# Two layers in split fp32: high and low halves joined into 512-column products, and a wider pace for layer b's attention

## The chip, the cores and the metric

The kernel runs on one core of a Trainium2 chip. The metric is the device time of one execution in microseconds (us). Engines: PE is TensorE (PEld its weight loads), DVE is VectorE, ACT is ScalarE, SP is SyncE, whose queue issues the transfers.

## What is computed

Two residual layers over 256 tokens of width 2048, 16 heads of 128. Layer a is latent attention, layer b block attention, which with 256 tokens is one causal block with a linear distance penalty.

```python
def reference(x, ...):
    for i in range(2):                       # layer a, then layer b
        y = mixer_i(rms_norm(x, norm_i)) @ w_out_i
        x = x + y
    return x

def moba_mixer(h, w_in, q_norm, k_norm):     # layer b
    q, k, v, gate = jnp.split(h @ w_in, 4, axis=-1)
    q, k = rms_norm(heads(q), q_norm), rms_norm(heads(k), k_norm)
    o = softmax(q @ k.T * scale - slope * distance, causal) @ v
    return from_heads(o) * jax.nn.silu(gate)
```

Layer a (`mla_mixer`) has the same form with low-rank projections for q, k and v, and a gate from its own input projection.

## The kernel before

All data is fp32. A product of fp32 accuracy is made of three fast ones: each operand is split into a high part (`fp32r`, ScalarE) and a low part (the rest, VectorE), and high x high, high x low and low x high are summed in PSUM. Weights arrive in tiles of 128 x 1024 (`wr`, 512 KB), which ScalarE turns into `wh` and VectorE into `wl`; four raw tiles, four high and three low ones are held. The tokens' parts lie in `xh` and `xl` (input chunks of 128 features x 256 tokens), those of the attention output in `ogh` and `ogl` (one chunk per head).

Two kinds of projection block exist. `blk_rows` keeps tokens stationary and streams 512 (or 384) weight columns: q, k and v. `blk_cols` keeps 128 weight columns stationary and streams the 256 tokens: gates and output projections. There, each 128 output columns and each input chunk take three products of 256 columns, and two such outputs share one PSUM bank. Five banks (`acc`) serve the blocks in turn, three (`w`) the attention pieces.

Layer b runs in four groups of four heads: gate, q, k and v blocks of 512 columns each, 16 steps per block. When q and k are done they are normalized and transposed (`flip`: a VectorE copy, a transposing DMA on SP's queue, a second VectorE copy). Each head has three steps: `s1` (scores `ps_s`, softmax: VectorE's reduction into `sm`, ScalarE's exponential, reciprocal `ri`, scaling of `sm`), `s2` (a flip of the probabilities through `pz`, then `ph`, `pl`, `p1`) and `s3` (product with v into `ps_o`, VectorE's `og` with the gate, then ScalarE's high and VectorE's low part). The group before runs its `s1` to `s3` between the products of the next group; the last group's stand between the products of the output projection, whose input chunk i needs head i. The blocks of columns 0 to 511 and 512 to 1023 go first: 12 steps of one and 6 of the other (heads 0 to 11 only), then the rest.

The order on every engine is fixed when the kernel is built. `ordered` walks the main list (projection steps) and the side list (attention steps) by estimated costs, lags and three PSUM banks, and takes whichever is ready; a step that takes a bank comes at the earliest `PACE` = 600 ns after the last such one. Each engine then runs its own instructions in that order. `token_scale` makes layer b's norm: `ps_st` sums squares, VectorE takes the inverse root in some fifteen small operations, `ps_r` spreads it over the rows; the gates' evictions need the result.

Of the kernel before, what the change touches and what calls it, by code (L numbers as in the profile page):

```python
# [28 lines left out]
P = 128  # L29
# [20 lines left out]
PACE = 600  # L50
# [42 lines left out]
def trunk(ctx: ExitStack, tc, xT, gains, cst, w_in_a, w_q_up, w_kv_up, w_out_a, w_in_b, w_out_b, outT):  # L93
# [60 lines left out]
    class Step:  # L154
# [3 lines left out]
        def __init__(self, fn, cost=0, lag=0, needs=(), after=(), w=None, bank=False):  # L158
            self.fn, self.cost, self.lag, self.w, self.bank = fn, cost, lag, w, bank
            self.needs, self.after, self.end = list(needs), list(after), None  # L160
# [6 lines left out]
    def ordered(main, side):  # L167
# [4 lines left out]
        while main or side:  # L172
            can = []
            for s in side + main[:1]:
                r = s.ready()
                if r is not None:
                    can.append((max(r, min(banks), last + PACE) if s.bank else r, s))
            r, s = next(((r, s) for r, s in can if r <= now), None) or min(can, key=lambda x: x[0])
            (main if main and s is main[0] else side).remove(s)
            now = max(now, r) + s.cost  # L180
            s.end = now
            if s.bank:
                banks[banks.index(min(banks))] = now + HOLD
                last = now
            out.append(s)
# [17 lines left out]
    def blk_rows(w, x, done, lag=PB, first=()):  # L203
# [4 lines left out]
        def go(wt, c, k):  # L208
            xh, xl = x()
# [13 lines left out]
    def blk_cols(w, x, done, lag=3000):  # L223
# [4 lines left out]
        def go(wt, c, k):  # L228
            xh, xl = x()
# [13 lines left out]
        return _steps(w, go, 3 * ns * 109, lag)  # L243

# [116 lines left out]
    def gate_done(g, rows):  # L361
        def done(a):
            for b in range(len(a)):
# [47 lines left out]
    def head_steps(h, scores, bias, vt, cost, needs, needs_v, after, lag, front):  # L411
# [176 lines left out]
    x_a = lambda: (xh, xl)  # L588
# [130 lines left out]
    def out_done_a(j):  # L719
        def f(a):  # L720
            xt = res["x"]
            c = 2 * j
            both = lines(xt[:, c:c + 2].rearrange("p a b -> p (a b)"))
            nc.vector.tensor_tensor(both, unpaired(a[0]), both, op=ALU.add)  # L724
# [12 lines left out]
    og = lambda: (ogh, ogl)  # L737
    outs_a = [blk_cols(w_out_a[:, 256 * j:256 * (j + 1)], og, out_done_a(j), 4000) for j in range(8)]
# [31 lines left out]
    def group_b(g):  # L770
# [63 lines left out]
        gate = blk_cols(w(3), x_b, gate_done(2 * g, rows_b))  # L834
# [7 lines left out]
        for h in range(4):  # L842
            hb.append(head_steps(4 * g + h, scores(h), bias(4 * g + h), lambda h=h: [x[:, h] for x in z["v"]],
                                 545, [tq, tk], v[-1:] + gate[-1:], [], S2B, nc.vector.tensor_copy))
        gate[-1].after += [h[2] for h in old] + [row_b]
# [4 lines left out]
        else:  # L850
            for i, s in enumerate(gate):
                s.needs.append(outs_a[i // 2][-1])
# [5 lines left out]
    def out_done_b(j):  # L858
        def f(a):
            xt = res["x"]  # L860
            for b in range(2):
                c = 4 * j + 2 * b
                y = xt[:, c:c + 2]
                both = lines(y.rearrange("p a b -> p (a b)"))
                nc.vector.tensor_tensor(both, unpaired(a[b]), both, op=ALU.add)  # L865
                nc.sync.dma_start(outT[c * P:(c + 2) * P].rearrange("(c p) t -> p c t", p=P), y)
        return f

    outs_b = [blk_cols(w_out_b[:, 512 * j:512 * (j + 1)], og, out_done_b(j)) for j in range(4)]
# [9 lines left out]
    main += outs_b[0][:12] + outs_b[1][:6] + outs_b[0][12:] + outs_b[1][6:] + outs_b[2] + outs_b[3]  # L879
# [62 lines left out]
```

## Time and profile before

| what | value |
|---|---|
| median of 3 runs | 756.62 us (755.7 to 757.58) |
| profiled execution | 756.45 us, span 754.7 us |
| TensorE busy | 745.3 us, 99% of the span |
| VectorE busy | 576.7 us, 76% |
| ScalarE busy | 488.7 us, 65% |
| TensorE clock granted | 0.999 of full speed |
| moved by DMA | 153.19 MB, 203 GB/s on average |

The span runs from the first to the last instruction of the program; the execution's own time is 1.75 us longer. Matmuls are pipelined, so busy time sums overlapping records: paces are read from start to start, or from the pieces of the chain that ended last.

### The profile page before, as it was taken

To read this page: it belongs to the slowest core of one execution; us is meant where nothing else is said; L and a number is where in the kernel's file an instruction comes from. 1 tells how busy PE (TensorE), PEld (TensorE's weight loads), DVE (VectorE), ACT (ScalarE), POOL (GpSimd) and SP (SyncE) were. 2 spreads that over 40 slices of the span, in tenths; PEclk is the share of its full clock that TensorE was granted. 3 is DMA by queue.
4 is the path that set the end of the run, shared out by engine and by line. 5 is a ranking of instruction groups with operands and counts; after the bars stand their busy time and mean duration, and the time that the engine had idled before them with its cause. 6 is when DMAs were issued, how large, how long until landed. Compare 5 with 4: busy or idle time off the path is not lost.

```text
span 754.7 us, 14125 instructions
## 1 busy us (share of the span) xinstructions
PE 745.3 (99%) x5246; PEld 707.1 (94%) x5246; DVE 576.7 (76%) x1207; ACT 488.7 (65%) x1025; POOL 0.2 (0%) x4
## 2 busy tenths in 40 slices
PE   8999999999999999999999999999999999999997
PEld 7999999999999999998889988998889988899997
DVE  6888899999998596765787767886788857887552
ACT  7767888888877575445666556675567666674331
POOL 0000000000000000000000000000000000000000
PEclk9999999999999999999999999999999999999999
DMA  9866666666657966666877768876787677877761
GB/s 296 263 182 182 169 184 161 184 170 158 182 178 192 280 209 211 195 181 211 227 224 187 194 216 228 246 187 195 203 237 219 190 215 214 235 197 219 232 223 43
DMA packets 137973, 153.19 MB, mean 203 GB/s; under 512 B 47280, under 2 KB 94768, under 8 KB 137904
## 3 DMA queue, kind: packets, MB, share of 16 engines
q1 hardware_dynamic: 137760, 152.27, 70.4%
q8 instruction: 41, 0.67, 0.4%
q14 instruction: 28, 0.23, 0.1%
q10 hardware_dynamic: 144, 0.02, 0.0%
HBM read 139.68 MB, written 2.10 MB: 188 GB/s over the span
## 4 chain that ended last, share of the span: by engine, by line
PE 91%; DVE 4%; DMA 2%; ACT 1%; issue 1%; SPq 0%; DVEq 0%; ACTq 0%
PE acc L198 84%; PE ps_s L198 4%; DVE wl L150 2%; PE ps_o L198 2%; PE ps_ta L201 1%; DMA c_sb<-cst 1%; DMA wr<-w_in_a 1%; ACT wh L146 1%; DMA sm<-pz 0%; ACT sq L542 0%; DVE xt L724 0%; SPq L132 0%; PE ps_lt L201 0%; DVE xt L865 0%; DVE xl L314 0%
## 5 line engine op out<-in xcount | busy, mean ns | idle before, releaser
L146 ACT ACTIVATE wh<-wr 128x1024 fp32r<-128x1024 f32 (+3 forms) x265 | 287.9, 1091 | 161.8 <-PE acc L198 134.9
L150 DVE TENSOR_TENSOR wl<-wr,wh 128x1024 fp32r<-128x1024 f32 (+3 forms) x265 | 314.3, 1189 | 90.3 <-PE acc L198 58.1
L198 PE MATMUL acc<-wh,xh 128*128 128x512 f32 (+1 forms) x448 | 169.0, 377 | 1.2 <-ACT wh L146 1.2
L198 PE MATMUL acc<-wl,xh 128*128 128x512 f32 (+1 forms) x448 | 167.7, 374 | 0.8 <-DVE wl L150 0.8
L198 PE MATMUL acc<-wh,xl 128*128 128x512 f32 (+1 forms) x448 | 167.4, 374 | 0.0
L198 PE MATMUL acc<-xh,wh 128*128 128x256 f32 x512 | 142.3, 278 | 0.0
L198 PE MATMUL acc<-ogh,wh 128*128 128x256 f32 x512 | 142.0, 277 | 0.0
L198 PE MATMUL acc<-ogh,wl 128*128 128x256 f32 x512 | 141.0, 275 | 0.3 <-DVE wl L150 0.2
L198 PE MATMUL acc<-xh,wl 128*128 128x256 f32 x512 | 140.8, 275 | 0.0
L198 PE MATMUL acc<-ogl,wh 128*128 128x256 f32 x512 | 140.8, 275 | 0.0
L198 PE MATMUL acc<-xl,wh 128*128 128x256 f32 x512 | 140.8, 275 | 0.0
L198 PEld LDWEIGHTS acc<-ogh,wl 128*128 128x128 f32 x512 | 98.3, 192 | 0.7 <-DVE wl L150 0.7
L198 PEld LDWEIGHTS acc<-xl,wh 128*128 128x128 f32 x512 | 98.2, 192 | 0.3
L198 PEld LDWEIGHTS acc<-xh,wh 128*128 128x128 f32 x512 | 98.2, 192 | 0.3
L198 PEld LDWEIGHTS acc<-xh,wl 128*128 128x128 f32 x512 | 98.3, 192 | 0.0
L198 PEld LDWEIGHTS acc<-ogl,wh 128*128 128x128 f32 x512 | 98.3, 192 | 0.0
L198 PEld LDWEIGHTS acc<-ogh,wh 128*128 128x128 f32 x512 | 98.3, 192 | 0.0
L198 PEld LDWEIGHTS acc<-wh,xh 128*128 128x128 f32 x448 | 85.0, 190 | 11.9 <-ACT wh L146 1.9
L198 PEld LDWEIGHTS acc<-wl,xh 128*128 128x128 f32 x448 | 84.9, 190 | 11.4 <-DVE wl L150 1.3
L198 PEld LDWEIGHTS acc<-wh,xl 128*128 128x128 f32 x448 | 84.8, 189 | 10.3
L198 PE MATMUL acc<-wh,xt 128*128 128x384 f32 (+1 forms) x192 | 57.5, 357 | 0.0
L426 ACT ACTIVATE sm<-sm,mn 128x128 f32<-128x128 f32 x64 | 29.0, 455 | 11.3 <-DVE mn L424 11.3
(154 smaller groups left out, 833.5 us busy)
## 6 DMA issues: line engine op xcount, KB each, us to landing
wr<-w_in_b SPq DMA_DIRECT2D x128, 512.0 KB, 4.3
wr<-w_in_a SPq DMA_DIRECT2D x32, 512.0 KB, 4.1
wr<-w_out_a SPq DMA_DIRECT2D x32, 512.0 KB, 4.5
wr<-w_out_b SPq DMA_DIRECT2D x32, 512.0 KB, 4.6
wr<-w_in_a SPq DMA_DIRECT2D x15, 416.0 KB, 5.2
wr<-w_q_up SPq DMA_DIRECT2D x16, 384.0 KB, 3.8
wr<-w_kv_up SPq DMA_DIRECT2D x8, 512.0 KB, 3.8
xt<-xT SPq DMA_DIRECT2D x4, 512.0 KB, 5.5
```

The lines of the kernel that those rows point to most:

```text
L146: nc.scalar.activation(self.ordering(self.h)[1], self.ordering(self.raw)[0], AF.Copy)
L150: nc.vector.tensor_tensor(self.ordering(self.l)[1], self.ordering(self.raw)[0], self.ordering(self.h.bitcast(F32))[1], op=ALU.subtract)
L198: chain(nc.tensor.matmul(*args, skip_group_check=True, **kw))
L201: chain(nc.tensor.transpose(*args))
L426: nc.scalar.activation(sm[:, sl], sm[:, sl], AF.Exp, bias=mn[:, t:t + 1], scale=-1.0, accum_out=rs[:, t:t + 1])
```

## The change

The tokens' high and low parts now lie side by side in one tile (`xhl`, `ohl`: 256 high columns, then 256 low ones). A new block, `blk_both`, streams both in one product of 512 columns with the high weights, and the high half alone with the low weights: two products for three, the same columns in all. An output of 128 columns now fills a PSUM bank, high half and low half apart, which are added when it is evicted (`gate_done` with `halves`, `added`). It is used for layer b's gates (in two pieces of 256 columns for one of 512), for the last four output pieces of layer a (pieces 4 to 7) and for the output columns 1024 to 1791 of layer b, whose last 256 columns stay with `blk_cols`. Layer b's attention steps get a pace of 3500 ns.

```diff
-        def __init__(self, fn, cost=0, lag=0, needs=(), after=(), w=None, bank=False):
+        def __init__(self, fn, cost=0, lag=0, needs=(), after=(), w=None, bank=False, pace=PACE):
...
-                    can.append((max(r, min(banks), last + PACE) if s.bank else r, s))
+                    can.append((max(r, min(banks), last + s.pace) if s.bank else r, s))
...
-PACE = 600
+PACE, PACEB = 600, 3500
...
+    def blk_both(w, x, done, lag=3000):
+        nk, ns = w.shape[0] // P, w.shape[1] // P
+        a = []
+
+        def go(wt, c, k):
+            hl = x()[2]
+            if k == 0:
+                a.extend(acc("acc") for _ in range(ns))
+            for s in range(ns):
+                ws = slice(s * P, (s + 1) * P)
+                last = k == nk - 1
+                matmul(a[s], wt.h[:, c, ws], paired(hl[:, k]), start=k == 0, stop=last)
+                matmul(a[s][:, :S], wt.l[:, c, ws], paired(hl[:, k, :S]), start=False, stop=last)
+            if k == nk - 1:
+                done(a)
+
+        return _steps(w, go, ns * 326, lag)
...
-    xh = one.tile([P, NC, S], F32R, name="xh")
-    xl = one.tile([P, NC, S], F32R, name="xl")
-    ogh = one.tile([P, H, S], F32R, name="ogh")
-    ogl = one.tile([P, H, S], F32R, name="ogl")
+    xhl = one.tile([P, NC, 2 * S], F32R, name="xhl")
+    ohl = one.tile([P, H, 2 * S], F32R, name="ohl")
+    xh, xl, ogh, ogl = xhl[:, :, :S], xhl[:, :, S:], ohl[:, :, :S], ohl[:, :, S:]
...
-                nc.vector.tensor_tensor(x, a[b].rearrange("p (h t) -> p h t", h=2),
-                                        rows().unsqueeze(1).to_broadcast([P, 2, S]), op=ALU.mult)
+                y = a[b].rearrange("p (h t) -> p h t", h=2)
+                if halves:
+                    y = x
+                    for h in range(2):
+                        z = a[2 * b + h]
+                        nc.scalar.copy(x[:, h], z[:, S:])
+                        nc.vector.tensor_tensor(x[:, h], z[:, :S], x[:, h], op=ALU.add)
+                nc.vector.tensor_tensor(x, y, rows().unsqueeze(1).to_broadcast([P, 2, S]), op=ALU.mult)
...
+    def added(a, xt, c):
+        both = xt[:, c:c + 2].rearrange("p a b -> p (a b)")
+        ys = [both] if len(a) == 1 else [xt[:, c], xt[:, c + 1]]
+        n = 2 * S // len(a)
+        for o in range(0, 2 * S, n):
+            for y, b in zip(ys, a):
+                nc.vector.tensor_tensor(lines(y), unpaired(b[:, o:o + n]), lines(y), op=ALU.add)
...
-        a = Step(s1, cost, S1, needs, bank=True)
+        a = Step(s1, cost, S1, needs, bank=True, pace=pace)
         b = Step(s2, 0, lag, [a])
-        return a, b, Step(s3, 545, S3, [b] + needs_v, after, bank=True)
+        return a, b, Step(s3, 545, S3, [b] + needs_v, after, bank=True, pace=pace)
...
-    outs_a = [blk_cols(w_out_a[:, 256 * j:256 * (j + 1)], og, out_done_a(j), 4000) for j in range(8)]
+    outs_a = [(blk_cols if j < 4 else blk_both)(w_out_a[:, 256 * j:256 * (j + 1)], og, out_done_a(j), 4000) for j in range(8)]
...
-        gate = blk_cols(w(3), x_b, gate_done(2 * g, rows_b))
+        gate = []
+        for i in range(2 * g, 2 * g + 2):
+            gate += blk_both(w_in_b[:, 3 * DM + 256 * i:3 * DM + 256 * (i + 1)], x_b, gate_done(i, rows_b, True))
...
-                                 545, [tq, tk], v[-1:] + gate[-1:], [], S2B, nc.vector.tensor_copy))
-        gate[-1].after += [h[2] for h in old] + [row_b]
+                                 545, [tq, tk], v[-1:] + gate[-1:], [], S2B, nc.vector.tensor_copy, PACEB))
+        for s in (gate[NC - 1], gate[-1]):
+            s.after += [h[2] for h in old] + [row_b]
...
-    outs_b = [blk_cols(w_out_b[:, 512 * j:512 * (j + 1)], og, out_done_b(j)) for j in range(4)]
+    outs_b = [(blk_both if 8 <= c < 14 else blk_cols)(w_out_b[:, c * P:(c + n) * P], og, out_done_b(c, 2 if 8 <= c < 14 else 1))
+              for c, n in ((0, 4), (4, 4), (8, 2), (10, 2), (12, 2), (14, 2))]
...
-    main += outs_b[0][:12] + outs_b[1][:6] + outs_b[0][12:] + outs_b[1][6:] + outs_b[2] + outs_b[3]
+    main += outs_b[0][:12] + outs_b[1][:6] + outs_b[0][12:] + outs_b[1][6:] + sum(outs_b[2:], [])
```

TensorE, first gate of layer b, where `ps_r` stands (before, 72 products after `ps_st`):

```order
L198 MATMUL acc<-xl,wh 128x256
L198 MATMUL acc<-xh,wl 128x256
L198 MATMUL ps_r<-diag,ones 128x256
L198 MATMUL acc<-xh,wh 128x256
L198 MATMUL acc<-xl,wh 128x256
L198 MATMUL acc<-xh,wl 128x256
```

After the change, 28 products after `ps_st`:

```order
L198 MATMUL acc<-xhl,wh 128x512
L198 MATMUL acc<-xhl,wl 128x256
L198 MATMUL ps_r<-diag,ones 128x256
L198 MATMUL acc<-xhl,wh 128x512
L198 MATMUL acc<-xhl,wl 128x256
L198 MATMUL acc<-xhl,wh 128x512
```

Three products of 256 became one of 512 and one of 256, and `ps_r` moved nearer to `ps_st`.

VectorE, last group of layer b, from the second copy of head 12's flip on (before; the `ISA` rows are the reductions of head 15's scores):

```order
L409 COPY pz<-sm 128x2x384
L429 RECIPROCAL ri<-rs 128x2
L431 TENSOR_SCALAR sm<-sm,ri 128x128
L431 TENSOR_SCALAR sm<-sm,ri 128x256
L424 ISA sm,mn<-ps_s,alibi 128x128
L424 ISA mn 128x1
L424 ISA sm,mn<-ps_s,alibi 128x256
L424 ISA mn 128x1
L440 TENSOR_TENSOR pl<-pz,ph 128x256
L150 TENSOR_TENSOR wl<-wr,wh 128x1024
L429 RECIPROCAL ri<-rs 128x2
L409 COPY pz<-sm 128x2x384
```

After the change, from the row behind the same copy to head 13's second copy (the reductions are head 14's):

```order
L463 RECIPROCAL ri<-rs 128x2
L150 TENSOR_TENSOR wl<-wr,wh 128x1024
L465 TENSOR_SCALAR sm<-sm,ri 128x128
L465 TENSOR_SCALAR sm<-sm,ri 128x256
L474 TENSOR_TENSOR pl<-pz,ph 128x256
L441 COPY pz<-sm 128x768
L150 TENSOR_TENSOR wl<-wr,wh 128x1024
L458 ISA sm,mn<-ps_s,alibi 128x128
L458 ISA mn 128x1
L458 ISA sm,mn<-ps_s,alibi 128x256
L458 ISA mn 128x1
L443 COPY pz<-sm 128x2x384
```

Before, the reductions of all four heads stand by the copies of heads 12 and 13; now head 13's first copy stands behind head 12's second one, and head 14's reduction behind that.

VectorE, a little further on, from the copies of heads 14 and 15 to head 12's output `og` (before):

```order
L440 TENSOR_TENSOR pl<-pz,ph 128x256
L407 COPY pz<-sm 128x768 x2
L150 TENSOR_TENSOR wl<-wr,wh 128x1024
L409 COPY pz<-sm 128x2x384
L150 TENSOR_TENSOR wl<-wr,wh 128x1024
L409 COPY pz<-sm 128x2x384
L150 TENSOR_TENSOR wl<-wr,wh 128x1024
L454 SCALAR_TENSOR_TENSOR og<-ps_o,gate 128x256
L440 TENSOR_TENSOR pl<-pz,ph 128x256
L456 TENSOR_TENSOR ogl<-og,ogh 128x256
```

After the change:

```order
L465 TENSOR_SCALAR sm<-sm,ri 128x128
L465 TENSOR_SCALAR sm<-sm,ri 128x256
L441 COPY pz<-sm 128x768
L443 COPY pz<-sm 128x2x384
L150 TENSOR_TENSOR wl<-wr,wh 128x1024
L443 COPY pz<-sm 128x2x384
L150 TENSOR_TENSOR wl<-wr,wh 128x1024
L488 SCALAR_TENSOR_TENSOR og<-ps_o,gate 128x256
L474 TENSOR_TENSOR pl<-pz,ph 128x256
L490 TENSOR_TENSOR ohl<-og,ohl 128x256
```

The first copies of heads 14 and 15 stood together ahead of both second ones; now head 15's first copy comes much later than head 14's (which is some ten rows further up), and a second copy follows at once. `og` of head 12 stands behind head 15's second copy in both.

On TensorE the four score pieces of the last group stand 12 products apart before and 36 after; from the last of them to the first output piece there are 120 and then 60, from the first output piece to the second 12 and then 24, from the second to the third 24 and then 12.

## Rows read from the trace of the kernel before

**Rows 1.** The page: busy time of each engine, its share of the span and instructions; and the share of each engine in the chain that ended last.

```profile
PE 745.3 (99%) x5246; PEld 707.1 (94%) x5246; DVE 576.7 (76%) x1207; ACT 488.7 (65%) x1025; POOL 0.2 (0%) x4
...
PE 91%; DVE 4%; DMA 2%; ACT 1%; issue 1%; SPq 0%; DVEq 0%; ACTq 0%
```

**Rows 2.** Pieces of the chain that ended last, in order of time: start in us, length in us, engine, tile, line and number of instructions. From layer b's norm to the end.

```profile
315.89 0.45 PE ps_st L198 x4
316.34 8.04 PE acc L198 x72
...
601.85 60.95 PE acc L198 x294
662.81 0.58 PE ps_s L198 x5
...
669.15 13.40 PE acc L198 x120
682.55 0.61 PE ps_o L198 x5
...
685.10 2.68 PE acc L198 x24
...
690.33 59.64 PE acc L198 x534
750.00 1.36 DVE xt L865 x2
```

**Rows 3.** Groups of instructions by line: output and inputs, shape, count, then busy us, mean ns of one, idle time ahead of them.

```profile
L397 DVE TENSOR_TENSOR vl<-acc,vh 128x256 fp32r<-128x256 f32 x8 | 3.4, 424 | 1.3 <-ACT vh L396 0.9
...
L724 DVE TENSOR_TENSOR xt<-acc,xt 128x512 f32<-128x512 f32 x8 | 5.5, 689 | 5.4 <-PE acc L198 5.4
...
L625 ACT COPY v<-acc 128x256 f32<-128x256 f32 x8 | 3.1, 394 | 0.0
```

**Rows 4.** One stretch, the first gate of layer b (311 to 333 us): busy time of each engine with its instructions, granted clock, share and rate of the DMA engines.

```profile
core 0: us, PE busy (x) PEld busy (x) DVE busy (x) ACT busy (x) POOL busy (x), PEclk, DMA share, GB/s
311.00:333.00 22.00, 22.00 (x195) 21.83 (x195) 14.95 (x33) 9.83 (x12) 0.00 (x0) 1.00 0.63 188
```

**Rows 5.** Instructions in order of time around layer b's norm, TensorE then VectorE: start us, length us, engine, line, operation, shapes, and idle time ahead in brackets.

```profile
315.73 0.61 PE L198 MATMUL ps_st<-ones,ssq 128*128 128x128 f32 x4
...
315.98 1.23 DVE L150 TENSOR_TENSOR wl<-wr,wh 128x1024 fp32r<-128x1024 f32 x1 [0.99 <-issue]
317.13 0.15 DVE L341 TENSOR_SCALAR rv_b<-ps_st 128x2 f32<-128x2 f32 x1
...
321.01 0.48 DVE L350 TENSOR_SCALAR diag<-c_sb,r_b 128x128 f32<-128x128 f32 x2
```

**Rows 6.** Two rows of the list of transfers (count, size, median us from issue to landing), then instructions in order of time in the last group of layer b: SyncE's transposes, VectorE (head 12's reduction first, then as the names say), and one of ScalarE.

```profile
wr<-w_out_b SPq DMA_DIRECT2D x32, 512.0 KB, 4.6
...
sm<-pz SPq DMA_TRANSPOSE x32, 3.4
...
667.20 1.22 SPq L408 DMA_TRANSPOSE sm<-pz  x1
...
669.87 1.22 SPq L408 DMA_TRANSPOSE sm<-pz  x1
...
676.32 2.68 SPq L408 DMA_TRANSPOSE sm<-pz  x2
...
664.04 0.28 DVE L424 CUSTOM_DVE_ANT_0 sm<-ps_s,alibi 128x128 f32<-128x128 f32 x1
...
665.39 0.17 DVE L429 RECIPROCAL ri<-rs 128x2 f32<-128x2 f32 x1 [0.71 <-ACT sm L426]
665.59 0.55 DVE L431 TENSOR_SCALAR sm<-sm,ri 128x128 f32<-128x128 f32 x2
...
666.61 0.56 DVE L407 COPY pz<-sm 128x768 uint16<-128x768 uint16 x1
...
669.96 0.61 DVE L409 COPY pz<-sm 128x768 uint16<-128x768 uint16 x1
...
671.12 0.28 DVE L424 CUSTOM_DVE_ANT_0 sm<-ps_s,alibi 128x128 f32<-128x128 f32 x1
...
671.67 0.42 DVE L440 TENSOR_TENSOR pl<-pz,ph 128x256 fp32r<-128x256 f32 x1
...
673.14 0.15 DVE L429 RECIPROCAL ri<-rs 128x2 f32<-128x2 f32 x1
673.32 0.61 DVE L409 COPY pz<-sm 128x768 uint16<-128x768 uint16 x1
...
675.74 1.02 DVE L407 COPY pz<-sm 128x768 uint16<-128x768 uint16 x2
...
681.24 0.61 DVE L409 COPY pz<-sm 128x768 uint16<-128x768 uint16 x1 [3.34 <-DMA sm<-pz]
...
684.49 0.41 DVE L454 SCALAR_TENSOR_TENSOR og<-ps_o,gate 128x256 f32<-128x256 f32 x1
...
685.41 0.43 DVE L456 TENSOR_TENSOR ogl<-og,ogh 128x256 fp32r<-128x256 f32 x1 [0.17 <-ACT ogh L455]
...
686.89 0.42 DVE L454 SCALAR_TENSOR_TENSOR og<-ps_o,gate 128x256 f32<-128x256 f32 x1
...
684.94 0.44 ACT L455 ACTIVATE ogh<-og 128x256 fp32r<-128x256 f32 x1 [1.41 <-DVE og L454]
```

More of the change, by code (lines that the diff above doesn't have):

```diff
@@ L154, in trunk @@
     class Step:
-        def __init__(self, fn, cost=0, lag=0, needs=(), after=(), w=None, bank=False):
-            self.fn, self.cost, self.lag, self.w, self.bank = fn, cost, lag, w, bank
+        def __init__(self, fn, cost=0, lag=0, needs=(), after=(), w=None, bank=False, pace=PACE):
+            self.fn, self.cost, self.lag, self.w, self.bank, self.pace = fn, cost, lag, w, bank, pace
             self.needs, self.after, self.end = list(needs), list(after), None
@@ L208, in go @@
         def go(wt, c, k):
-            xh, xl = x()
+            xh, xl = x()[:2]
             if k == 0:
@@ L228, in go @@
         def go(wt, c, k):
-            xh, xl = x()
+            xh, xl = x()[:2]
             if k == 0:
@@ L359, in trunk, with gate_done @@
     gate_of = {}
-    def gate_done(g, rows):
+    def gate_done(g, rows, halves=False):
         def done(a):
-            for b in range(len(a)):
+            for b in range(len(a) // 2 if halves else len(a)):
                 ub = wk.tile([P, 2, S], F32, tag="gate", name="gate", bufs=4)
@@ L409, in flip, with head_steps @@
         nc.vector.tensor_copy(words(b), planes(a))
-    def head_steps(h, scores, bias, vt, cost, needs, needs_v, after, lag, front):
+    def head_steps(h, scores, bias, vt, cost, needs, needs_v, after, lag, front, pace=PACE):
         st = {}
@@ L586, in kr_t @@
         parts(ps, 1.0, krf, *lat_st["kr"], True)
-    x_a = lambda: (xh, xl)
+    x_a = lambda: (xh, xl, xhl)
     rows_a = lambda: scale_a["rows"]
@@ L722, in f @@
             c = 2 * j
-            both = lines(xt[:, c:c + 2].rearrange("p a b -> p (a b)"))
-            nc.vector.tensor_tensor(both, unpaired(a[0]), both, op=ALU.add)
+            added(a, xt, c)
             split_x(c, G_NB)
@@ L736, in trunk @@
     rx2 = one.tile([P, 2], F32, name="rx2")
-    og = lambda: (ogh, ogl)
-    outs_a = [blk_cols(w_out_a[:, 256 * j:256 * (j + 1)], og, out_done_a(j), 4000) for j in range(8)]
+    og = lambda: (ogh, ogl, ohl)
+    outs_a = [(blk_cols if j < 4 else blk_both)(w_out_a[:, 256 * j:256 * (j + 1)], og, out_done_a(j), 4000) for j in range(8)]
     for g in range(8):
@@ L851, in group_b @@
             for i, s in enumerate(gate):
-                s.needs.append(outs_a[i // 2][-1])
+                s.needs.append(outs_a[i % NC // 2][-1])
         turns_of.extend([[tq], [tk]])
@@ L856, in group_b, with out_done_b @@
         return gate + q + k + v
-    def out_done_b(j):
+    def out_done_b(c0, m):
         def f(a):
             xt = res["x"]
[L861 to L866, printed above, removed]
-        return f
-    outs_b = [blk_cols(w_out_b[:, 512 * j:512 * (j + 1)], og, out_done_b(j)) for j in range(4)]
+            for b in range(0, len(a), m):
+                c = c0 + 2 * b // m
+                added(a[b:b + m], xt, c)
+                nc.sync.dma_start(outT[c * P:(c + 2) * P].rearrange("(c p) t -> p c t", p=P), xt[:, c:c + 2])
+        return f
+    outs_b = [(blk_both if 8 <= c < 14 else blk_cols)(w_out_b[:, c * P:(c + n) * P], og, out_done_b(c, 2 if 8 <= c < 14 else 1))
+              for c, n in ((0, 4), (4, 4), (8, 2), (10, 2), (12, 2), (14, 2))]
     col_b, row_b = token_scale(ssq_b, "b", scale_b, [outs_a[7][-1]], scales_b)
```

## The prediction

> **What bounds the kernel now.** I read the busy shares and the chain that ended last, then the chain piece by piece, then VectorE's and SyncE's own order at the end of the last head group. TensorE is busy for 99% of the span and 91% of the chain is its own work [rows 1]. So a product saved is time saved, unless something new makes TensorE wait. From the start of layer b on it hardly waits: the pieces of the chain follow each other with no other engine between them until the last output block is added [rows 2].
>
> The paces come from the pieces. 534 products of 256 columns take 59.64 us, 111.7 ns each. In the piece of 294, the last 24 are output products of 256 columns (2.68 us by the piece x24); the other 270 have 512 columns and take (60.95 - 2.68) / 270 = 215.8 ns [rows 2]. Per column that is 0.436 ns at 256 and 0.4215 ns at 512. The reader is to see that a 256-wide product pays 3.8 ns over 256 x 0.4215 = 107.9 ns, and that this is all that wide products can give back.
>
> **The products that are joined.** Now a block of 128 outputs and one input chunk take three products of 256 columns, 335.1 ns. After the change they are one of 512 and one of 256. There are 16 x 16 such triples in the gates, 8 x 16 in the last four output pieces of layer a, 6 x 16 in the output of layer b, 480 in all. The columns stay the same.
> - Nearest rows: the two steady paces, 215.8 + 111.7 = 327.5 ns, 7.6 ns less, 3.65 us in all. I take this one.
> - Upper bound: the extra of the 256 goes too (768 x 0.4215 = 323.7 ns), 5.5 us.
> - Lower bound: each product that follows a 256-wide one still pays 3.8 ns, the wide one too (331.3 ns), 1.8 us. A loss is excluded, since no product gets columns and both paces are of this kernel.
>
> The Trainium skill ("TensorE: Matmul & The Clock Gate", Back-to-back issue gap) gives columns / 2.4 GHz plus 2.5 ns for a warm product that stands alone: 109.2 ns at 256, 215.8 ns at 512. The second is this trace's pace, the first is not (111.7 ns), so the measurement decides. By the page on both sides a join would be worth only the 2.5 ns of the product that goes, an estimated 1.2 us, and it speaks against the change.
>
> **The added evictions.** A gate pair now takes two ScalarE copies of 128x256 and two VectorE adds of 128x256 before its product with the scale; an output pair of the new kind takes four adds of 256 instead of one of 512. From the nearest rows, 0.394 us a copy and 0.424 us an add [rows 3]: 16 x 0.394 = 6.3 us on ScalarE, 16 x 0.424 + 7 x (4 x 0.424 - 0.689) = 13.8 us on VectorE, spread over 15 pieces. In the first gate stage VectorE is busy 14.95 us of 22 and ScalarE 9.83 [rows 4], so the idle parts cover them; uncovered, one eviction costs its 1 to 1.5 us once. PSUM: a joined pair holds two of the five banks for 16 x 2 x 0.3275 = 10.5 us, and each bank is wanted again 10.5 us after its last product at the earliest; a 1.5 us eviction fits. In layer a's output stage VectorE's weight splits are already late now and then, so I put 0.2 us (0 to 0.3) there.
>
> **The token scale's wait.** Between the sum for layer b's scale (ps_st) and the product that spreads it (ps_r), VectorE works a chain of small operations. Now 72 products, 8.04 us, cover it [rows 2]. The first gate piece is half as long after the change, its end must come after ps_r, and the order puts 14 joined triples, 14 x 0.3275 = 4.6 us, between the two. In the trace the chain's last operation ends at 321.01 + 0.48 = 321.49, and gate products begin at 316.34 less the 0.16 by which a product starts ahead of its piece of the chain (315.73 against 315.89 for ps_st), so the wait is 321.49 - 316.18 - 4.6 = 0.7 us [rows 2, 5]. It would be 0 if the 1.23 us weight split ahead of the chain stood elsewhere; the order leaves it there.
>
> **The pacing.** In groups 0 to 2 a later start of a head's pieces is covered: behind them lie the next group's products (60.95 us between the last output and the next score piece [rows 2]). In the last group nothing but the output blocks' first 18 steps is left, and these are now spent earlier: 36 products between score pieces instead of 12, then 60, then 24 between the first two output pieces. Right after the second one stands the first product that needs head 12's output; now 24 more filler products stand there, and no wait is seen. Counted from the start of the first score piece (662.81 - 0.16 = 662.65), TensorE gets there after 192 x 0.1117 + 4 x 0.58 + 2 x 0.61 = 25.0 us.
>
> VectorE is what is late. It takes its operations in order, and in the new order head 12's output (og) stands behind head 15's second copy of the flip, as it does now. But now heads 14 and 15 flip together (675.74, two copies, two transposes, one wait), and after the change each flip has a wait of its own. The walk, in us after 662.65, from [rows 6] (b is the copy behind the transpose):
> - Head 12: reciprocal at 2.74, scaling 0.55 and more, first copy from 3.5 to 4.1 (nothing of head 13 stands between any more). A transpose that is alone lands 2.76 us after its issue (667.20 to 669.96) or 3.45 (669.87 to 673.32): b12 at 6.9.
> - From b12, copy 0.6, reciprocal, weight split 1.2, scaling 0.55, pl 0.4, first copy 0.56 make 3.3 with their overlaps, then the transpose: b13 6.1 to 6.75 later.
> - From b13 the same up to head 14's first copy (2.7), then head 15's reductions 0.5 later, its reciprocal 1.35 to 2.0 behind them (664.04 to 665.39, 671.12 to 673.14), split, scaling, copy 2.5, transpose 2.8 to 3.45: b15 9.8 to 11.1 later.
> - Copy and weight split 1.8, og and ScalarE's high part 0.89 (684.49 to 684.94 + 0.44): 2.5 to 2.7.
>
> Sum 25.3 to 27.5 against 25.0: TensorE waits 0.3 to 2.5, I take the middle, 1.4. Then the low part comes 0.45 us behind the high one (685.38 to 685.84) where a product wants it after 0.11: some 0.35 for three of the four heads. Heads 13 and 15 add 0.1 and 0.3, since og follows og every 2.4 us (684.49, 686.89) and TensorE needs 12 x 0.1117 + 0.61 + 0.35 = 2.3 a head. Together 1.5 (1.0 to 1.8), so the end of the group costs 2.9 us (1.3 to 4.3). On SyncE each transpose takes 1.22 us of its queue, between weight loads; a load that starts that much later is still in time, since four tiles of 8 x 0.335 = 2.7 us are under way and one lands in 4.6.
>
> **The sum.** The profiled execution took 756.45 us, 1.75 over its span of 754.7 and 0.17 under the median of 756.62. -3.65 + 0.2 + 0.7 + 2.9 = +0.15: 756.6 us.
>
> **Rivals.**
> - *The joins give little.* The wide product behind a 256-wide one pays the 3.8 ns as well: -1.8 + 3.8 = +2.0, 758.4 us. For it: every product behind a 256 pays it now. Against it: in the steady 512 rows it is absent. By the page's formula for both widths it would be -1.2 + 3.8, an estimated 759.0.
> - *Faster.* The joined pair runs at the 512 pace throughout (-5.5) and the lone transposes land in 2.76 (0.3 + 1.5 at the group's end): -5.5 + 0.7 + 1.8 = -3.0, 753.4 us. For it: few products then follow a narrow one. Against it: weight splits and transposes share the DMA engines, and the second lone one took 3.45.
> - *Slower, by one mechanism: the transposes in a row.* Three flips now stand one behind another ahead of head 12's output, so each us that a transpose takes longer costs three. The pair of heads 14 and 15 took 4.92 (676.32 to 681.24). Over the middle of 3.1 by 0.7, at 3.8, it passes 0.3%; at 4.3 the price is 3.6 more, 760.2 us. For it: a weight load is often under way when a transpose is issued, and the median landing over all 32 is 3.4 [rows 6]. Against it: the two lone ones of this group.
> - *The joins do nothing:* the pace per column stays that of 256. +3.8, 760.2 us. Only a 512-wide operand that runs unlike those in the trace would do that.
>
> **How the numbers follow.** Chances: the forecast 0.45, little from the joins 0.14, faster 0.24, transposes 0.12, nothing from the joins 0.05. 0.3%, about what a measurement of this kernel tells from no change, is 2.3 us: 754.3 to 758.9. I put a tenth of the forecast below that, a quarter of the faster case inside it, and a fifth of the first rival above it. Faster: 0.045 + 0.18 = 0.23; within: 0.405 + 0.06 + 0.11 = 0.57; slower: 0.03 + 0.12 + 0.05 = 0.20. The forecast's own range, with the end of the group at 1.3 to 4.3, the scale's wait at 0 to 0.8 and the evictions at 0 to 0.3, is 754.1 to 758.2. Reaching to the faster case below and half way into the slow ones above, the range is 753.6 to 759.6.
>
> **What would show it.** TensorE's count falls by 480. In the chain, the pieces of the gates give the pace of a joined pair: 327.5 ns confirms the first term, 331 the first rival, 324 the faster case. ps_r should wait 0.7 us for VectorE's diag. In the last 90 us output products should wait for ohl, first some 1 to 2 us for ScalarE's high part of head 12, then in steps of 0.35 for VectorE. VectorE should show four separate waits on sm<-pz. I am wrong if those waits lie elsewhere: at weight splits in the gates, or at score pieces in groups 0 to 2.

## The result and the profile after

The changed kernel takes 761.25 us (median of 6) where the kernel before takes 756.16 us in the same comparison: ratio 1.0055, interval 1.0038 to 1.0072: slower by 5.1 us in the medians and by about 4 by the ratio. The forecast of 756.6 us, and its range up to 759.6, were wrong.

The profiled execution took 759.19 us, span 757.4, 2.7 us over the span of before; it is the fastest of the six. So its trace holds 2.7 of the 5 us; a second profile comes with the experiments.

The page: busy time of TensorE, and each engine's share of the chain that ended last.

```profile
PE 743.4 (98%) x4766; PEld 690.5 (91%) x4766; DVE 588.3 (78%) x1244; ACT 491.9 (65%) x1041; POOL 0.2 (0%) x4
...
PE 80%; DVE 8%; DMA 7%; ACT 3%; issue 2%; SPq 0%; DVEq 0%; ACTq 0%
```

TensorE has its 480 products less. But of the chain it has 80% where it had 91% [rows 1]; the transfers' share went from 2 to 7%, VectorE's from 4 to 8%. These are waits. Some of the chain's pieces say where (start, length, engine, tile, line, count):

```profile
319.63 0.81 PE ps_r L198 x2
...
396.27 3.93 PE acc L198 x24
...
595.73 5.82 DMA sm<-pz
...
602.06 0.68 DVE gx L393
602.74 1.14 DVE wl L150
603.92 2.64 PE acc L198 x11
...
661.65 0.57 PE ps_s L198 x5
...
665.60 2.74 DMA sm<-pz
...
671.50 4.36 DMA sm<-pz
...
679.15 7.41 DMA sm<-pz x2
687.13 1.21 DVE wl L150
...
696.13 57.07 PE acc L198 x419
753.22 0.69 DVE xt L405
```

Twelve joined pairs take 3.93 us, 327.5 ns a pair: the price that the prediction took. Before, pieces of TensorE alone led from layer b's norm to the end [rows 2]. Now transposes stand in the chain at two places: ahead of group 3's q block (595.73) and, in three pieces, the four of the last group. TensorE's own rows there, in order of time, with the idle time and its releaser in brackets:

```profile
319.63 0.81 PE L198 MATMUL ps_r<-diag,ones 128*128 128x256 f32 x2 [0.48 <-DVE diag L369]
...
603.92 0.48 PE L198 MATMUL acc<-wl,xhl 128*128 128x512 f32 x1 [1.08 <-DVE wl L150]
...
689.20 0.84 PE L198 MATMUL acc<-ohl,wh 128*128 128x256 f32 x2 [2.59 <-ACT ohl L489]
...
691.60 0.84 PE L198 MATMUL acc<-ohl,wh 128*128 128x256 f32 x2
...
695.67 0.84 PE L198 MATMUL acc<-ohl,wh 128*128 128x256 f32 x2 [0.17 <-ACT ohl L489]
```

The brackets understate the loss, since the end of a product is modelled; from start to start, 2.89 us lie ahead of 689.20 where 0.11 would do, 1.46 ahead of 603.92 for 0.22, 0.75 ahead of ps_r for 0.11. VectorE's rows at the two places, the copy behind each transpose (`pz<-sm` at line 443) above all:

```profile
601.57 0.60 DVE L443 COPY pz<-sm 128x768 uint16<-128x768 uint16 x1 [2.47 <-DMA sm<-pz]
602.06 0.68 DVE L393 TENSOR_TENSOR gx<-gx,rr_b 128x512 f32<-128x512 f32 x1
602.65 1.22 DVE L150 TENSOR_TENSOR wl<-wr,wh 128x1024 fp32r<-128x1024 f32 x1
...
668.43 0.61 DVE L443 COPY pz<-sm 128x768 uint16<-128x768 uint16 x1 [0.82 <-DMA sm<-pz]
...
675.95 0.61 DVE L443 COPY pz<-sm 128x768 uint16<-128x768 uint16 x1 [2.79 <-DMA sm<-pz]
...
683.36 0.62 DVE L443 COPY pz<-sm 128x768 uint16<-128x768 uint16 x1 [0.61 <-DMA sm<-pz]
...
686.64 0.60 DVE L443 COPY pz<-sm 128x768 uint16<-128x768 uint16 x1 [1.57 <-DMA sm<-pz]
687.13 1.21 DVE L150 TENSOR_TENSOR wl<-wr,wh 128x1024 fp32r<-128x1024 f32 x1
688.26 0.42 DVE L488 SCALAR_TENSOR_TENSOR og<-ps_o,gate 128x256 f32<-128x256 f32 x1
```

The four waits of VectorE that the prediction foresaw are there, and head 12's output (688.26) stands behind the last of them. At 601.57 VectorE stands 2.47 us at such a copy, and behind it in its queue is the weight split that TensorE then waits for.

The two spans, cut at the first 256-wide score product of each group (read from the traces, us):

| stretch | before | after | after, were there no new wait |
|---|---|---|---|
| start to group 0's scores | 397.78 | 395.68 | 395.67 + ps_r's wait |
| group 0's to group 1's | 88.33 | 87.90 | 87.84 |
| group 1's to group 2's | 88.34 | 87.83 | 87.85 |
| group 2's to group 3's | 88.34 | 90.22 | 88.50 |
| group 3's to the last product | 87.57 | 91.28 | 86.84 |
| last product to the end | 4.31 | 4.49 | |

The last column takes 7.6 ns off for each joined triple (192, 64, 64, 64 and 96 of them), and moves 1,536 columns, 0.65 us, from the first stretch to the fourth, where the order now puts them. Against it the last group costs 4.44 us, the turn from group 2 to 3 costs 1.72 (1.24 of it, 1.46 less 0.22, is the wait at 603.92), and ps_r 0.74, which the rest of the first stretch gives back, 0.43 of it ahead of anything that was changed (214.53 us to layer a's first output product, 214.96 before).

### The profile page after: what moved, and what is told of

The parts are those of the page before. It is cut to its first block, busy times and chain, and to the rows that moved or that the text cites. A ratio compares the mean times of both kernels' runs of the same rounds, so it can differ in the third digit from the quotient of the medians.

```text
span 757.4 us, 13191 instructions
## 1 busy us (share of the span) xinstructions
PE 743.4 (98%) x4766; PEld 690.5 (91%) x4766; DVE 588.3 (78%) x1244; ACT 491.9 (65%) x1041; POOL 0.2 (0%) x4
## 4 chain that ended last, share of the span: by engine, by line
PE 80%; DVE 8%; DMA 7%; ACT 3%; issue 2%; SPq 0%; DVEq 0%; ACTq 0%
PE acc L198 74%; DMA sm<-pz 5%; DVE wl L150 4%; PE ps_s L198 3%; PE ps_o L198 1%; DMA c_sb<-cst 1%; ACT wh L146 1%; PE ps_ta L201 1%; DMA wr<-w_in_a 1%; DVE sm L465 0%; DVE pz L443 0%; DVE xt L405 0%; ACT sq L576 0%; DVE pz L441 0%; DVE pl L474 0%
## 5 line engine op out<-in xcount | busy, mean ns | idle before, releaser
L198 PE MATMUL acc<-wh,xhl 128*128 128x512 f32 (+1 forms) x896 | 265.8, 375 | 0.9 <-ACT wh L146 0.9
L198 PEld LDWEIGHTS acc<-wh,xhl 128*128 128x128 f32 x896 | 168.9, 189 | 21.9 <-ACT wh L146 1.6
L198 PE MATMUL acc<-ohl,wh 128*128 128x256 f32 (+1 forms) x800 | 173.1, 307 | 3.0 <-ACT ohl L489 2.8
L198 PE MATMUL acc<-xhl,wh 128*128 128x256 f32 (+1 forms) x768 | 173.6, 313 | 0.0
L198 PE MATMUL acc<-wl,xhl 128*128 128x512 f32 (+1 forms) x448 | 167.8, 375 | 1.9 <-DVE wl L150 1.9
L198 PE MATMUL acc<-ohl,wl 128*128 128x256 f32 x512 | 140.4, 274 | 0.3 <-DVE wl L150 0.3
L198 PE MATMUL acc<-xhl,wl 128*128 128x256 f32 x512 | 140.3, 274 | 0.1
L198 PEld LDWEIGHTS acc<-ohl,wh 128*128 128x128 f32 x800 | 130.3, 191 | 10.0 <-ACT ohl L489 3.2
L198 PEld LDWEIGHTS acc<-xhl,wh 128*128 128x128 f32 x768 | 126.3, 191 | 6.6
L198 PEld LDWEIGHTS acc<-ohl,wl 128*128 128x128 f32 x512 | 98.3, 192 | 0.6 <-DVE wl L150 0.6
```

The source lines that it names most:

```text
L198: chain(nc.tensor.matmul(*args, skip_group_check=True, **kw))
```

## The experiments

Each comparison with the kernel before is of runs on one chip. The two runs of one and the same kernel (`pace_early`) on different chips have ratios 0.4% apart, so small differences are read within one comparison, or in the stretches of the traces. Here are all of them, same cuts as above:

| kernel | us | ratio to before [interval] | 0 to 1 | 1 to 2 | 2 to 3 | 3 to last product |
|---|---|---|---|---|---|---|
| joins_only | 758.09 | 1.0019 [1.0001, 1.0036] | 89.11 | 89.26 | 90.75 | 86.84 |
| pace_only | 766.21 | 1.0111 [1.0089, 1.0132] | 90.17 | 89.74 | 89.37 | 95.41 |
| pace_early | 753.90 | 0.9949 [0.9933, 0.9965] | 87.87 | 87.87 | 88.58 | 86.83 |
| pace_last | 763.25 | 1.0073 [1.0055, 1.0091] | 88.98 | 88.70 | 91.20 | 90.95 |
| after_again | 760.83 | 1.0062 [1.0043, 1.0081] | 88.05 | 87.87 | 89.94 | 91.63 |
| more_cover | 754.34 | 0.9975 [0.9959, 0.9992] | 87.82 | 87.83 | 90.62 | 86.83 |
| unjoined | 759.72 | 1.0045 [1.0029, 1.0061] | 90.48 | 89.85 | 89.41 | 87.55 |
| qfirst | 755.10 | 0.9976 [0.9964, 0.9988] | 88.40 | 87.87 | 89.31 | 86.84 |
| pace_early_again | 755.61 | 0.9989 [0.9976, 1.0002] | 87.83 | 88.11 | 89.42 | 86.85 |
| pace_1500 | 753.85 | 0.9975 [0.9964, 0.9986] | 87.84 | 87.85 | 88.55 | 86.85 |
| act_queue | 793.70 | 1.0496 [1.0453, 1.0539] | 95.29 | 93.50 | 96.00 | 96.68 |
| pool_copy | 755.73 | 0.9988 [0.9974, 1.0002] | 87.83 | 87.83 | 88.54 | 88.61 |
| pace_1500_qfirst | 752.18 | 0.9936 [0.9915, 0.9957] | 87.84 | 87.84 | 88.57 | 86.83 |

### The two parts apart, and the pace by groups

joins_only is the change with the old pace, pace_only the kernel before with the new one, pace_early and pace_last the change with the new pace in some groups only:

```diff
-PACE, PACEB = 600, 3500
+PACE, PACEB = 600, 600
```

That is joins_only; this is pace_early (pace_last has `g == 3` in it, pace_only the kernel before with the lines of the change that carry the pace):

```diff
-                                 545, [tq, tk], v[-1:] + gate[-1:], [], S2B, nc.vector.tensor_copy, PACEB))
+                                 545, [tq, tk], v[-1:] + gate[-1:], [], S2B, nc.vector.tensor_copy, PACEB if g < 3 else PACE))
```

> The change with the pace of layer b's attention steps left at 600 ns: only the joined products remain. The profiled execution of the changed kernel lost 4.3 us in the last head group and 1.5 us at the turn from group 2 to group 3, and 0.75 us at the wait of ps_r. Theory A (the pacing costs all of that but the last, the joins give the 3.65 us of the prediction): -3.65 + 0.75, some 753.5 us, ratio 0.996, and no wait over 0.5 us in the last group. Theory B (the joins give no more than 1.8 us, and their evictions cost some of it): 756 to 757 us, ratio 1.00. Theory C (without the pace the joined steps put score pieces 4 triples apart instead of 12 products, VectorE comes late in groups 0 to 2): 755 to 757 us, with TensorE's waits in groups 0 to 2.

> The kernel before with the pace of 3500 ns alone, no joined product. Theory A: 756.4 + 4.3 + 1.5 or more, 761 to 764 us, ratio 1.006 to 1.010; TensorE waits 2 us or more for head 12's output and VectorE's copies behind the transposes take four waits of their own. Theory B (the pacing costs the 2.9 us of the prediction): 759 to 760 us.

> The change with the pace of 3500 ns in groups 0 to 2 and 600 in the last. Theory A: the last group's 4.3 us go, what the pace costs in groups 0 to 2 stays: joins_only + 1.5 to 3.5 us, 755 to 757 us. Theory B (groups 0 to 2 are covered): the same as joins_only. Theory C (without the pace groups 0 to 2 are too dense): faster than joins_only.

> The change with the pace of 3500 ns in the last group alone. Theory A: joins_only + 4.3 us, some 757.8 us, with one wait of 2 to 3 us for head 12's output and five of 0.35. Theory B (the last group costs 2.9): joins_only + 2.9 us.

The last group is as theory A says: its stretch is 86.83 to 86.84 us wherever the old pace stands there, and 90.95 to 91.63 with the new one, 4.1 to 4.8 more; pace_only, without joins, loses 7.8 there, part of it to the clock (below). By the ratios, on one chip, pace_last stands 0.54% over joins_only.

Some times lay outside what had been named for them: joins_only at 758.09 us (755 to 757 by theory C), pace_only at 766.21 (761 to 764), pace_last 5.2 us over joins_only (4.3), and further down qfirst at 755.10 (753.0) and pace_early_again at 755.61 (753 to 755). The theories are told apart by the stretches of the traces.

The waits in joins_only are theory C's. It is not faster than before, though its last group has no wait and its products cost 3.65 us less. TensorE's waits from 395 to 615 us in it (engine, line, what it waited for: total us, times, longest):

```profile
PE acc L198 <- DVE wl L150: 2.4, 3, 1.5
PE ps_o L198 <- DVE pl L474: 0.9, 3, 0.5
```

With joined steps half as long, a pace of 600 ns puts the score pieces 4 products, two pairs, apart: 0.66 us, where 12 products of 256, 1.34 us, stood before. VectorE's weight splits and low parts then come late: the three groups take 4.8 us more (89.11, 89.26, 90.75 against 87.87, 87.87, 88.58 in pace_early), 3.3 of it in the waits of these two rows. So the wider pace in groups 0 to 2 is worth about 0.7% by the ratios, 4.2 us by the medians. pace_early is the first kernel that is clearly faster than before in its comparison; run once more on another chip (pace_early_again) its interval reaches 1.0002. In the kernel before, the same pace does harm there as well: pace_only waits 2.7 us for weight splits in that window, then 3.9 us for head 12's high part (waits of 395 to 615 us and of 680 to 712 us, then TensorE from 695.76 to 702.59 us: length, busy time with its instructions, granted clock, share and rate of the DMA engines):

```profile
PE acc L198 <- DVE wl L150: 2.7, 4, 0.9
...
PE acc L198 <- ACT ogh L455: 3.9, 2, 3.7
...
695.76:702.59 6.83, 6.34 (x28) 0.50 0.50 159
```

The granted clock falls to 0.50, its 1.2 GHz level, within that wait and stays there for 6.83 us, which costs about 3 us (an estimate: half of the 6.34 us busy). With the wait of 3.9 this is most of the 7.8 us that pace_only's last group lost.

### Once more, with cover, with the joins undone, and with ps_r covered

after_again is the changed kernel itself. more_cover, on the changed kernel:

```diff
-    main += outs_b[0][:12] + outs_b[1][:6] + outs_b[0][12:] + outs_b[1][6:] + sum(outs_b[2:], [])
+    main += outs_b[0][:12] + outs_b[1][:12] + outs_b[0][12:] + outs_b[1][12:] + sum(outs_b[2:], [])
```

unjoined, on pace_early:

```diff
-                matmul(a[s], wt.h[:, c, ws], paired(hl[:, k]), start=k == 0, stop=last)
+                matmul(a[s][:, :S], wt.h[:, c, ws], paired(hl[:, k, :S]), start=k == 0, stop=False)
+                matmul(a[s][:, S:], wt.h[:, c, ws], paired(hl[:, k, S:]), start=k == 0, stop=last)
```

qfirst, on pace_early, with the needs of group 0's first block moved from the gate to q:

```diff
-        return gate + q + k + v
+        return gate + q + k + v if g else q + gate + k + v
```

> The changed kernel once more, on the chip of the next three, and with a profile of its own: its first profiled execution was the fastest of six. Theory A (the pacing's cost lies in VectorE's waits for transposes, whose landing differs from execution to execution): 759 to 762 us, a wait of 2.5 to 4 us for head 12's output, and waits for weight splits in groups 0 to 2 at other places than in the first profile or of another size. Theory B (the cost lies elsewhere, in a stage without such waits): the same waits, and the rest of the 4 to 5 us spread over the pace of the products.

> The change with twelve steps of the second output block, not six, ahead of the first product that needs head 12: 72 products of 256 columns more, 8.0 us of cover, the pace of 3500 ns kept. Theory A (the cover is what the pacing used up): the wait for head 12's output and the steps of 0.35 us behind it vanish, 4.3 us or more less than after_again, 755 to 757 us. Theory B (three transposes in a row, or VectorE's own order, stop TensorE wherever the products stand): the wait stays at over 1 us, 759 us or more.

> pace_early (the change with the pace of 3500 ns in groups 0 to 2 alone) with the joined product taken apart: the same tiles, banks, evictions and order, but three products of 256 columns for one of 512 and one of 256, in all 480 places. The difference to pace_early is the joins and nothing else. By the steady paces (335.1 against 327.5 ns) 3.65 us more than pace_early's 753.9, some 757.5 us. By the lower bound 1.8 us more, 755.7; by the page's formula 1.2 us more, 755.1.

> pace_early with the first head group's q block ahead of its gate, so that 36 products of 512 columns (7.8 us) stand between ps_st and ps_r instead of 28 in joined pairs (4.6 us). Theory A (the wait of ps_r for VectorE's chain, with what follows it, is 0.7 to 1.1 us of the changed kernel's time): 753.0 us, and no wait at ps_r. Rival (the wait only moves, to the first weight split or eviction behind it): 753.9 us as pace_early.

unjoined leaves the first chunk's high by high product of each output out of the sum; the products, their sizes and their order on TensorE are those named. On VectorE and SyncE the order is not pace_early's: around the last flip of each of the groups 0 to 2, copies, weight splits and a weight load stand elsewhere. So the whole times differ by more than the joins.

after_again loses at the same two places: 1.44 us above 88.50 at the turn to group 3 and 4.79 above 86.84 in the last group. But the second loss is made up otherwise. TensorE's wait for head 12 (start to start 2.13 us, where 0.11 would do) is 2.0 us and not 2.8, below the 2.5 to 4 that theory A named; behind it the clock fell (the row of the wait, then TensorE in three stretches, columns as above):

```profile
690.91 0.86 PE L198 MATMUL acc<-ohl,wh 128*128 128x256 f32 x2 [1.82 <-ACT ohl L489]
...
688.48:691.59 3.11, 1.21 (x8) 1.00 0.57 181
691.59:695.00 3.41, 3.41 (x18) 0.50 0.77 238
695.00:698.00 3.00, 3.00 (x28) 1.00 0.17 64
```

18 products in the middle stretch and 28 in the shorter one behind it: at 0.50 a product of 256 columns takes 0.215 us, where 0.112 is the pace before. That costs some 1.7 us (an estimate: half of 3.41). So theory A holds for the places; the size is in part the clock, which neither theory named. The span is 760.2 us, and 2.6 us of what it has over the first profile lie ahead of layer a's output products (217.16 for 214.53 us), which the change does not touch; there too the clock stood at 0.50, from 12.34 to 15.75 us.

more_cover decides on the cover: the last group's stretch falls to 86.83 us, the time falls by 6.5 us in the same comparison, and the pace is still 3500 ns. (Its profiled execution took 759.27 us, 4.9 over the median; in it the turn to group 3 lost 2.1 us, at 90.62.) In its chain TensorE's pieces follow one another past the place where head 12 was waited for:

```profile
680.84 6.70 PE acc L198 x60
687.54 0.61 PE ps_o L198 x5
688.15 4.02 PE acc L198 x36
692.16 0.61 PE ps_o L198 x5
692.77 4.02 PE acc L198 x36
```

unjoined prices the join. Its pieces of three products a triple (group 1, then the end):

```profile
488.21 4.02 PE acc L198 x36
...
694.40 60.31 PE acc L198 x540
```

and the same two in pace_1500, which has the joins (the first with six pairs):

```profile
484.84 1.97 PE acc L198 x12
...
688.19 59.59 PE acc L198 x444
```

12 triples take 4.02 us, 335 ns each, against 3.93 us for 12 pairs; the end's 96 triples take 0.72 us more, 7.5 ns each. So the steady paces hold, 3.65 us for 480. The whole kernel lost more than these, 0.6 to 1.0% against the two comparisons of pace_early, which are on other chips: its first three turns are 4 us over what they would be without waits, and its four waits there are all at weight splits. Whether the other order on VectorE makes them, or the unjoined steps themselves, stays open.

qfirst takes the wait of ps_r away: its product then starts on time and not 0.64 us late. From layer a's first output product to group 0's scores it took 180.9 us, pace_early 181.5: 0.6 us, where 0.9 were expected. The other profiles with the gate ahead and joined products took 181.0 to 181.6 (but 183.7 in more_cover's and 191 in act_queue's), so one profile gives 0.1 to 0.8; the whole time, 755.10 us, does not show it.

### The pace between, the other queue, the other engine

pace_early_again is pace_early. pace_1500 is pace_early with another number, pace_1500_qfirst has qfirst's edit too:

```diff
-PACE, PACEB = 600, 3500
+PACE, PACEB = 600, 1500
```

act_queue and pool_copy are the changed kernel with one line of `flip` each (in pool_copy `back` is GpSimd's copy for layer b's heads, VectorE's elsewhere):

```diff
-        nc.sync.dma_start_transpose(a.bitcast(U16).rearrange("p (c t) -> p c t", t=P), b.bitcast(U16))
+        nc.scalar.dma_start_transpose(a.bitcast(U16).rearrange("p (c t) -> p c t", t=P), b.bitcast(U16))
```

```diff
-        nc.vector.tensor_copy(words(b), planes(a))
+        back(words(b), planes(a))
```

> The kernel of pace_early once more, for a second profile and beside the next two on one chip: 753 to 755 us, no wait in the last group, and between 0 and 2 us of waits for weight splits at the turn from group 2 to 3, as the transposes land.

> pace_early with 1500 ns for 3500 in groups 0 to 2: score pieces stand 12 joined products apart there (6 pairs of 327.5 ns, 1.97 us), not 24 (3.93 us) and not 4 (0.66 us, joins_only); before the change they stood 12 products, 1.34 us, apart. Theory A (joined steps need more products between the pieces only to keep before's distance in time; wider costs nothing gained): the same as pace_early or up to 1 us faster, no wait over 0.5 us in groups 0 to 2. Theory B (each transpose must land before the next is issued, so that VectorE waits at no copy for long): waits of 0.5 to 1.7 us in groups 0 to 2 as in joins_only, 756 us or more.

> The changed kernel, pace 3500 ns in all groups, with all flips' transposes issued on ScalarE's queue instead of SyncE's, where they stand between weight loads. Theory A (the lone transposes land in 3.8 to 4.4 us for 2.7 because they wait behind weight loads in SyncE's queue): landings of 2.7 to 3 us, the wait for head 12's output falls from 2 to 2.8 us to under 0.5, 757 us or less. Theory B (they share the DMA engines with loads under way, whichever queue): landings as in after, and ScalarE, 1.2 us busy with each issue, makes its copies late: 761 us or more.

> The changed kernel, pace 3500 ns in all groups, with the second copy of layer b's head flips (the one that waits for the transpose) on GpSimd, which is idle otherwise, instead of VectorE. The waits for transposes leave VectorE's queue; what is left there of each flip is pl, two operations later in the chain. Theory A (og of head 12 is late because VectorE, in order, stands at three copies that wait for lone transposes): the wait for head 12's output falls from 2 to 2.8 us to under 1 us, and the waits for weight splits at the turn from group 2 to 3 go: 757 us or less. Theory B (pl passes the wait on, or GpSimd's copy takes 2 us or more for 0.6): the wait stays over 2 us, 761 us or more.

> pace_1500 (1500 ns in groups 0 to 2, 600 in the last) with the first group's q block ahead of its gate: the parts that won, together. No wait at ps_r, none over 0.5 us in the groups or at the end: pace_1500's 753.9 less 0.6 us (the stretch from the first output product of layer a to group 0's first score piece was 180.9 us in qfirst and 181.5 in pace_early), 753.2 us. Rival: the q block's weight splits come late behind the norm's chain, and it gives nothing: 753.9.

pace_1500 has no wait in any group: theory A. 1.97 us between score pieces are enough, and 3.93 buy nothing. By its ratio it is 0.14% under pace_early_again beside it, which lost 0.8 us at one weight split at the turn to group 3; the two intervals overlap.

act_queue answers the question of the queue, against theory A. Transposes issued by ScalarE land no sooner (issue group: count, median us to landing), first in the changed kernel, then in act_queue:

```profile
sm<-pz SPq DMA_TRANSPOSE x32, 3.9
```

```profile
sm<-pz ACTq DMA_TRANSPOSE x32, 4.1
```

Before it was 3.4 [rows 6]. So standing behind weight loads in SyncE's queue is not what makes transposes slow; that they share the DMA engines with loads under way is left, argued and not shown. ScalarE's order also suffered: every group lost 5 to 10 us, some of it to the clock, which stood at 0.50 for 24 us in all.

pool_copy takes the copies that wait for a transpose out of VectorE's queue, and both waits go: the weight splits at the turn to group 3 are no longer late (88.54 us for 90.22), and head 12's output is ready when TensorE comes. It does not do that alone. TensorE's order is that of the changed kernel, but on SyncE the transposes of a group stand elsewhere between the weight loads, other instructions of VectorE and ScalarE moved as well, and the transposes land sooner (median 3.3 us, for 3.9). That a copy which waits holds up what stands behind it is read from VectorE's rows of the changed kernel: the late split (602.65) and head 12's output (688.26) stand behind such copies. pool_copy agrees, but does not separate this from transposes that land sooner.

GpSimd and VectorE, then TensorE, in the last group:

```profile
666.37 2.00 POOL L443 COPY pz<-sm 128x768 uint16<-128x768 uint16 x1 [69.25 <-DVE ri L463]
...
683.82 1.07 POOL L443 COPY pz<-sm 128x768 uint16<-128x768 uint16 x1 [5.92 <-DMA sm<-pz]
...
667.37 1.29 DVE L465 TENSOR_SCALAR sm<-sm,ri 128x128 f32<-128x128 f32 x2
...
682.25 0.42 DVE L488 SCALAR_TENSOR_TENSOR og<-ps_o,gate 128x256 f32<-128x256 f32 x1
...
683.87 2.04 DVE L150 TENSOR_TENSOR wl<-wr,wh 128x1024 fp32r<-128x1024 f32 x1 [0.27 <-PE acc L198]
...
684.17 0.49 PE L198 MATMUL acc<-ohl,wh 128*128 128x256 f32 x2
...
686.76 0.84 PE L198 MATMUL acc<-ohl,wh 128*128 128x256 f32 x2 [0.37 <-ACT ohl L489]
```

`og` of head 12 comes at 682.25, before the last flip's copy (683.82) instead of behind it, and the wait of 2.8 us is 0.1 (684.17). The steps of 0.35 us behind it stay, and one of 0.56 at head 13, where a split next to GpSimd's copy took 2.04 us: 1.77 us in all over 86.84. The time went to 0.9988 of before, from 1.0055 and 1.0062.

pace_1500_qfirst puts the winning parts together: 752.18 us, ratio 0.9936 [0.9915, 0.9957]. No wait at ps_r, none over 0.2 us in the groups. It beats the kernel before, and by the ratios the changed one (1.0055, 1.0062).

## Why the prediction was wrong

- **The joins: right.** -3.65 us by the steady paces. Twelve pairs in 3.93 us, and stretches shorter by 0.49 us for 64 triples and by 0.73 for 96, give 7.6 ns a triple. The two bounds, the rival of joins that give little and that of joins that give nothing are out. The estimate by the Trainium skill's formula ("TensorE: Matmul & The Clock Gate", Back-to-back issue gap), 1.2 us in all, does not agree with 7.6 ns a triple: that is 3.65.
- **ps_r: right.** The product starts 0.64 us late, and the one behind it 0.1 later than before: 0.74, forecast 0.7.
- **The evictions: not contradicted.** 0.2 us were forecast; no wait in a trace points to them, and a cost of that size could not be seen.
- **The last group: the mechanism right, the size wrong.** 4.44 us (4.79 in the second profile, some 1.7 of them by the clock), where 2.9 were taken out of 1.3 to 4.3. The walk from the first score product (661.65 - 0.16 = 661.49): b12 at 6.9 as forecast; b13 7.5 later, forecast 6.1 to 6.75; b15 10.7 after that, inside 9.8 to 11.1; then 2.6 to TensorE's start, as forecast. The sum of 27.7 lies just past the upper end of 27.5, TensorE came at 24.9 (forecast 25.0), and the wait was 2.8. The step that failed is the price of a lone transpose: 2.76 to 3.45 from the two rows of before. Read from issue to copy they took 2.8, 4.45, 4.2 and 3.9 now; head 13's 4.45 alone put b13 past its range. The third rival, the transposes in a row, named this, with 3.8 as the point from which it decides. Its counter-argument was a sample of two, while the median over all 32 stood in the same rows at 3.4. But the price did not come three times, as that rival had it: the sum is 1.3 us over its middle of 26.4, 1.1 of it at b13 and 0.25 at b15, though the last two transposes were late as well. (Where another rival has weight splits share the DMA engines with transposes, weight loads must be meant: the splits are VectorE's.)
- **Groups 0 to 2 covered: wrong.** This step priced the pacing at nothing, because the next group's products cover the heads' output. That output is indeed never waited for. But in the same queue as the copy that waits for a transpose stand weight splits for the products that were to be the cover. At 601.57 a transpose of 5.8 us holds VectorE for 2.5 us and TensorE loses 1.24. The turn cost 1.72 us and 1.44 in the two profiles of the changed kernel. pace_early, more_cover and qfirst have the same order on every engine between 500 and 640 us, and there it cost 0.08 and 0.92 (two profiles), 2.12 and 0.81: at one and the same order the price differs from execution to execution, and the three dearest are those where group 2's last transpose took 5.8 to 6.0 us, for 5.3 to 5.5 in the other three. What was said would make the prediction wrong, a wait at a weight split in groups 0 to 2, is what happened, in group 3's q block, where group 2's heads run.
- **The rest.** The profile's own time was forecast as 0.15 us above that of before, and was 2.74 above. The last group (+1.54) and the turn to group 3 (+1.72) are more than that difference; the stretch up to group 0's scores gives some 0.7 back, as said above. That the median is 2.1 us above the profiled run cannot be laid to a place; but the other five executions were granted 0.996 to 0.998 of the clock, the profiled one 0.999, and after_again shows two places where such time can go. The prediction had no term for the clock.

A thing that the prediction did not ask: what the joins would cost at the old pace. They make steps half as long, and a pace in ns that was hidden behind a step of 1.34 us becomes the limit. joins_only shows it: 4.8 us in three groups, more than the joins give.

## What to carry to other kernels

A wait for a transfer on an engine that works in order is not paid by the result it waits for alone: list what stands behind it in the queue, and who waits for that. Where several such transfers stand in a row, price each at the median of all of them rather than at the best rows nearby. When steps get shorter, look again at every rule that spaces them in time. And where TensorE waits, read the granted clock of the stretch behind the wait too: the wait may not be its whole price.

## What was not expected of the hardware

- TensorE's clock fell to 0.50 at a wait for an attention output in three profiles (waits of 2.0 us in after_again, 3.9 in pace_only, some 5 in act_queue) and not in two others (2.8 in the changed kernel, 2.5 in pace_last). Why in the one and not in the other is not shown.
- A copy on GpSimd (128x768, 16 bit) took 1.05 to 1.07 us, and up to 2.00; VectorE's neighbours in time stretched: the scaling pair 1.29 us for 0.55 [rows 6], the weight split 2.04 for 1.22. The Trainium skill ("SBUF — State Buffer", SBUF: two separate sides) says that VectorE and GpSimd share a pair of ports that one instruction holds to its end. These rows agree roughly: the split began 0.05 us after a copy of 1.07 and took 0.82 longer, and the copy of 2.00 began at 666.37, 0.14 after a split of 1.22.
- The place of a transpose's issue, SyncE's or ScalarE's queue, moved its median landing by 0.2 us only (3.9 and 4.1), while transposes of one kind spread from 2.74 to 5.82 us in one trace.
